# Chunk 14 of an MLP's second product as seven block products too, with two weight sums of chunks 13 and 14 made by accumulating transfers

## The chip, the core and the metric

The kernel runs on one NeuronCore of a Trainium2 chip. The metric is the device time of one execution in microseconds. TensorE (PE) multiplies 128x128 blocks into the banks of PSUM; VectorE (DVE) and ScalarE (ACT) do elementwise work; GpSimd (POOL) and SyncE (SP) issue transfers (DMA). Each engine takes its own instructions strictly in the order in which the program lists them, and waits at one whose inputs are not there.

## The reference

One layer of a decoder trunk over 256 rows of 1024: an input projection, a conformer convolution and a sparse attention, a cross attention, a squared-ReLU MLP and a last RMSNorm. What the change touches is the end:

```python
    hf = _rmsnorm(h, norm_ffn_g[l]) @ w_ff1[l]
    h = h + jnp.square(jax.nn.relu(hf)) @ w_ff2[l]
return _rmsnorm(h, norm_final_g)
```

`w_ff1` is 1024x4096, `w_ff2` 4096x1024, all float32.

## The kernel before

**Precision.** Every weight and activation is split into a high part (ACT copies it in a shorter float format, names `hi...`) and a low part (DVE subtracts the high one, names `lo...`). A product is three matmuls: high by high, high by low, low by high (`mm3`, line 382).

**The MLP.** It runs over 16 chunks of 256 hidden columns. For chunk c, the first product (`f1`, function `first`, line 1312) is made in two halves ("sides") of 128 columns into a bank `ps_f`; then ACT and DVE make the hidden part: relu, square, differences, high and low (`activation`, line 1225; tiles `ft` for the values, `fs` for high and low). The second product (`f2`) adds its share to the banks `ps_p`, named "1" to "7", which stay open over all chunks. The first product runs two chunks ahead of the second.

**Seven or eight block products.** The second product of a chunk is a 2x2 by 2x2 product of blocks (two groups of 128 rows, two of 128 hidden columns, two of 512 output columns), so eight block products of three 512-wide matmuls. For the chunks in `SEVEN` (1 to 13) it is done with seven, in Strassen's manner: the weights enter as four groups, "left" (two blocks as loaded), "last" (one block), "outer" and "inner" (two sums each), and the hidden part enters with three differences more. The weight sums (tiles `sums`) are made by DVE in `seven` (line 242): `outer()` adds one block to two others in one operation of 1024 elements, `inner(2)` and `inner(3)` add a block each, 512 elements, to what is there. `TERMS` (line 1304) says which weight block goes with which hidden part into which bank. At the end the banks are combined ("bank sums", tiles `comb`) and added to the rows `h_rm` ("residuals", `add_to` and `last_residual`).

**The end.** Chunks 14 and 15 (`JOINED` = 14) are done as eight plain products together, bank by bank, in `last_products` (line 1408), so that each bank is finished in turn: bank 2, 3, 4, then 5 and 1 with 256 columns each. Behind each bank DVE adds the residual, ACT squares and sums it (`last_squares`), and `last_norm` scales a block of 128 rows and issues its output.

**What sets the order.** The order is written by hand, as the program is recorded. Splits stand in a list of jobs (`last_jobs`, line 215): `split_high` records the next job's ACT part, `split_low` the next DVE part; `weights` calls both until the group that a product needs is there. Generators (`activation` among them) advance one step at each `tick()`; `done()` ticks until a hidden part is recorded. A job's high part may only be recorded while the pools `highs` and `lows` (6 tiles each) have room; some groups use tiles of the pool `t8` (12 tiles, taken in turn) in their place. Weights come in order on SP's queue (`load`, `fetch`): the next chunk's when a chunk's tile is released.

In names, the number in `hi80left` counts the stream's chunks: 78 is `f2` chunk 12, 80 chunk 13, 81 chunk 14 and 82 chunk 15.

## Time and profile before

| | |
|---|---|
| time, median of three runs (lowest to highest) | 501.92 us (501.77 to 502.3) |
| the profiled execution's own time, and its span | 501.92 us, 500.1 us |
| PE busy over the span | 490.9 us, 3120 matmuls |
| DVE busy | 465.4 us, 847 instructions |
| ACT busy | 349.1 us, 606 instructions |
| POOL busy | 30.7 us, 47 instructions |
| granted TensorE clock, mean | 0.997 |

The span goes from the first to the last instruction; the time of the run holds some work around it. Busy time of PE is modelled, since matmuls overlap, so stages are judged by what each engine waited for. In timelines a row gives the start, the busy time, the engine, the line, the operation with output and input, how many equal instructions it merges (x), and, in brackets, idle time of the engine before it with what ended it. Line 81 is the helper that records PE's and DVE's instructions (82 after the change), so tiles tell more than lines.

### The profile page before, as it was taken

To read this page: it belongs to the slowest core of one execution; us is meant where nothing else is said; L and a number is where in the kernel's file an instruction comes from. 1 tells how busy PE (TensorE), PEld (TensorE's weight loads), DVE (VectorE), ACT (ScalarE), POOL (GpSimd) and SP (SyncE) were. 2 spreads that over 40 slices of the span, in tenths; PEclk is the share of its full clock that TensorE was granted. 3 is DMA by queue.
4 is the path that set the end of the run, shared out by engine and by line. 5 is a ranking of instruction groups with operands and counts; after the bars stand their busy time and mean duration, and the time that the engine had idled before them with its cause. 6 is when DMAs were issued, how large, how long until landed. Compare 5 with 4: busy or idle time off the path is not lost.

```text
span 500.1 us, 8286 instructions
## 1 busy us (share of the span) xinstructions
PE 490.9 (98%) x3120; PEld 442.7 (89%) x3120; DVE 465.4 (93%) x847; ACT 349.1 (70%) x606; POOL 30.7 (6%) x47
## 2 busy tenths in 40 slices
PE   7999999999999999999999999999999999999995
PEld 5999998888888888888889999988999999999984
DVE  5999899999999789999988997799999999999996
ACT  7657777787856666767846567687777677777753
POOL 2002212221111100000000000000000000000000
PEclk9999999999999999999999999999999999999998
DMA  8959678899887653345655553766766456654412
GB/s 315 381 190 276 176 191 266 234 250 272 245 224 217 183 174 110 147 169 173 248 169 186 219 185 115 264 186 136 192 241 214 170 185 207 241 207 171 134 78 84
DMA packets 28376, 100.35 MB, mean 201 GB/s; under 512 B 10784, under 2 KB 11552, under 8 KB 19376
## 3 DMA queue, kind: packets, MB, share of 16 engines
q1 hardware_dynamic: 24416, 93.03, 54.7%
q0 software_dynamic: 3632, 6.59, 7.4%
q8 instruction: 24, 0.39, 0.3%
q10 hardware_dynamic: 288, 0.20, 0.1%
q14 instruction: 16, 0.13, 0.1%
HBM read 91.16 MB, written 1.05 MB: 184 GB/s over the span
## 4 chain that ended last, share of the span: by engine, by line
PE 85%; DVE 9%; ACT 3%; issue 1%; DMA 1%; POOL 0%; DVEq 0%; SPq 0%; ACTq 0%; POOLq 0%
PE ps_f L81 18%; PE ps_p L81 13%; PE ps_conv L81 10%; PE ps_ao L81 5%; PE ps_q L81 4%; PE ps_k L81 4%; PE ps_ga L81 4%; PE ps_gc L81 4%; PE ps_v L81 4%; PE ps_xo L81 3%; PE ps_qi L81 2%; PE ps_xk L81 2%; PE ps_xv L81 2%; DVE lo L81 2%; PE ps_xq L81 2%; DVE gc_t L81 1%
## 5 line engine op out<-in xcount | busy, mean ns | idle before, releaser
L81 DVE TENSOR_TENSOR lo<-raw,hi 128x1024 fp32r<-128x1024 f32 x133 | 161.2, 1215 | 3.4 <-ACT hi L295 3.0
L295 ACT ACTIVATE hi<-raw 128x1024 fp32r<-128x1024 f32 x133 | 138.5, 1047 | 2.4 <-DMA raw<-in_wst_dram 2.4
L81 PE MATMUL ps_f<-ff_p,hi 128*128 128x256 f32 (+1 forms) x464 | 92.5, 294 | 0.0
L81 PEld LDWEIGHTS ps_f<-ff_p,hi 128*128 128x128 f32 x464 | 75.3, 191 | 3.7
L81 DVE SCALAR_TENSOR_TENSOR acc<-u,cw,acc 128x234 f32<-128x234 f32 (+29 forms) x190 | 78.0, 461 | 0.3
L81 PE MATMUL ps_f<-ff_p,lo 128*128 128x256 f32 x256 | 71.3, 282 | 0.0
L81 PEld LDWEIGHTS ps_f<-ff_p,lo 128*128 128x128 f32 x256 | 48.9, 191 | 0.5
L81 PE MATMUL ps_conv<-n_p,hi 128*128 128x256 f32 x224 | 40.9, 285 | 0.0
L81 PEld LDWEIGHTS ps_conv<-n_p,hi 128*128 128x128 f32 x224 | 34.8, 192 | 0.9 <-issue 0.7
L81 PE MATMUL ps_conv<-n_p,lo 128*128 128x256 f32 x112 | 31.7, 283 | 0.0
L623 POOL DMA_DIRECT2D acc<-products x25 | 21.7, 867 | 125.6 <-ACT products L622 47.6
L273 ACT ACTIVATE inner<-sums 128x1024 fp32r<-128x1024 f32 x13 | 13.8, 1061 | 20.6 <-DVE sums L81 20.6
L81 PE MATMUL ps_q<-n_p,hi 128*128 128x512 f32 x64 | 23.6, 406 | 0.0
L81 PE MATMUL ps_k<-n_p,hi 128*128 128x512 f32 x64 | 23.5, 407 | 0.0
L81 PE MATMUL ps_ao<-o_p,hi 128*128 128x512 f32 x64 | 22.6, 401 | 0.0
L81 PE MATMUL ps_co<-u_p,hi 128*128 128x512 f32 (+1 forms) x80 | 22.2, 351 | 0.0
L81 PE MATMUL ps_mix<-mix_p,hi 128*128 128x512 f32 (+1 forms) x80 | 22.2, 351 | 0.0
L81 PE MATMUL ps_ga<-n_p,hi 128*128 128x512 f32 x64 | 22.0, 396 | 0.0
L81 PE MATMUL ps_gc<-n_p,hi 128*128 128x512 f32 x64 | 22.0, 396 | 0.0
L622 ACT ACTIVATE products<-u,cw 128x231 f32<-128x231 f32 (+24 forms) x50 | 21.9, 488 | 0.0
L81 PEld LDWEIGHTS ps_conv<-n_p,lo 128*128 128x128 f32 x112 | 21.5, 192 | 0.0
L81 PE MATMUL ps_p<-outer,fs 128*128 128x512 f32 x78 | 20.1, 393 | 0.0
(424 smaller groups left out, 1243.8 us busy)
## 6 DMA issues: line engine op xcount, KB each, us to landing
raw<-in_wst_dram SPq DMA_DIRECT2D x67, 1024.0 KB, 5.6
raw<-in_wst_dram SPq DMA_DIRECT2D x28, 512.0 KB, 4.4
acc<-products POOLq DMA_DIRECT2D x25, 256.0 KB, 6.8
x_rm<-in_x_dram SPq DMA_DIRECT2D x2, 512.0 KB, 4.1
mem_rm<-in_mem_dram SPq DMA_DIRECT2D x1, 1024.0 KB, 9.0
mem_t<-in_memt_dram SPq DMA_DIRECT2D x1, 1024.0 KB, 11.0
h_t<-in_xt_dram SPq DMA_DIRECT2D x1, 1024.0 KB, 7.1
raw_f<-in_wst_dram SPq DMA_DIRECT2D x1, 1024.0 KB, 9.5
```

The lines of the kernel that those rows point to most:

```text
L81: return fn(*args, **kwargs)
L273: act(hi, src, AF.Copy)
L295: act(hi, raw[:, ns], AF.Copy)
L622: act(prod[:, a, s:], u[:, t, : S - s], AF.Copy, scale=cw[:, t, TAPS - 1 - s : TAPS - s])
L623: nc.gpsimd.dma_start(acc[:, ts, :], prod, accum_op=ALU.add)
```

## The change

Chunk 14 joins `SEVEN`, and only chunk 15 is left for `last_products`. Chunk 13's and 14's products are interleaved: after chunk 15's first side come left, inner and outer of 13, then left, inner and outer of 14, then chunk 15's second side, then "last" of 13 and of 14. For both chunks the outer sums are no longer made by DVE: when the chunk's weights are fetched, POOL issues two transfers from DRAM, one that copies two blocks into `sums` and one that adds the third block to both (`accum_op`). The inner sums stay on DVE, in the order inner before outer. The high and low parts of the two chunks' sums go to the pools `highs` and `lows`. Chunk 15's raw weights get a `t8` tile of their own. The bank sums are spread: one ahead of "last" of 14, the others between the residuals of banks 2 and 3.

ACT's order ahead of the first products of chunk 14, before the change (`ft`, `fs` are hidden parts, `raw` weights as loaded, `both` chunk 15's weight parts; the rows go from the relu of chunk 14's second side on):

```order
L1203 ACTIVATE ft_5203<-ps_f_5255 128x256
L1232 ACTIVATE ft_5203<-ft_5203 128x512
L273 ACTIVATE outer_5288<-sums_5246 128x1024
L1210 ACTIVATE fs_5202<-ft_5203 128x512
L295 ACTIVATE hi_1_5301<-raw_3546 128x1024
L273 ACTIVATE inner_5318<-sums_5246 128x1024
L295 ACTIVATE hi_0_5327<-raw_5191 128x1024
L295 ACTIVATE hi_1_5335<-raw_5191 128x1024
L1203 ACTIVATE ft_5312<-ps_f_5333 128x256
L1217 ACTIVATE ft_5312<-ft_5312 128x256
L1391 ACTIVATE comb_5315<-ps_p_4008 128x512
```

and now, from chunk 13's inner high part on:

```order
L281 ACTIVATE hi80inner<-sums_5082 128x1024
L1212 ACTIVATE ft_5209<-ps_f_5260 128x256
L1241 ACTIVATE ft_5209<-ft_5209 128x512
L281 ACTIVATE hi80outer<-sums_5082 128x1024
L281 ACTIVATE hi81left<-raw_5194 128x1024
L281 ACTIVATE hi81inner<-sums_5196 128x1024
L1212 ACTIVATE ft_5319<-ps_f_5324 128x256
L1226 ACTIVATE ft_5319<-ft_5319 128x256
L281 ACTIVATE hi81outer<-sums_5196 128x1024
L1219 ACTIVATE fs_5208<-ft_5209 128x896
L1219 ACTIVATE fs_5318<-ft_5319 128x256
```

The inner high part of each chunk now stands ahead of the next relu and of the outer high part, and the hidden-14 part (`fs_5208`) is recorded behind chunk 14's outer high part.

DVE's order at the same place, before, from chunk 13's outer sum on:

```order
L81 TENSOR_TENSOR sums_5246<-raw_5080 128x1024
L81 TENSOR_TENSOR fs_5091<-ft_5092,fs_5091 128x896
L81 TENSOR_TENSOR lo80last<-raw_5080,hi80last 128x512
L81 TENSOR_TENSOR lo_0_5258<-raw_3546,hi_0_5257 128x1024
L81 TENSOR_TENSOR sums_5246<-sums_5246,raw_5080 128x512
L81 TENSOR_TENSOR outer_5288<-sums_5246,outer_5288 128x1024
L81 TENSOR_TENSOR sums_5246<-sums_5246,raw_5080 128x512
L81 TENSOR_TENSOR fs_5202<-ft_5203,fs_5202 128x512
L81 TENSOR_TENSOR lo_1_5302<-raw_3546,hi_1_5301 128x1024
L81 TENSOR_TENSOR inner_5318<-sums_5246,inner_5318 128x1024
L81 TENSOR_TENSOR lo_0_5328<-raw_5191,hi_0_5327 128x1024
L81 TENSOR_TENSOR lo_1_5336<-raw_5191,hi_1_5335 128x1024
```

and now, from the low part of chunk 15's first-side weights (`lo_0`) on:

```order
L82 TENSOR_TENSOR lo_0_5242<-raw_3546,hi_0_5241 128x1024
L82 TENSOR_TENSOR sums_5082<-sums_5082,raw_5080 128x512
L82 TENSOR_TENSOR fs_5094<-ft_5095,fs_5094 128x896
L82 TENSOR_TENSOR lo80left<-raw_5080,hi80left 128x1024
L82 TENSOR_TENSOR sums_5082<-sums_5082,raw_5080 128x512
L82 TENSOR_TENSOR lo80inner<-sums_5082,hi80inner 128x1024
L82 TENSOR_TENSOR ft_5209<-ft_5209 128x256
L82 TENSOR_TENSOR lo80outer<-sums_5082,hi80outer 128x1024
L82 TENSOR_TENSOR sums_5196<-sums_5196,raw_5194 128x512
L82 TENSOR_TENSOR ft_5209<-ft_5209 128x128
L82 TENSOR_SCALAR minus<-ms_ff 128x2
L82 TENSOR_TENSOR lo81left<-raw_5194,hi81left 128x1024
```

followed by:

```order
L82 TENSOR_TENSOR sums_5196<-sums_5196,raw_5194 128x512
L82 TENSOR_TENSOR ft_5209<-ft_5209 128x128
L82 TENSOR_TENSOR lo81inner<-sums_5196,hi81inner 128x1024
L82 TENSOR_TENSOR lo81outer<-sums_5196,hi81outer 128x1024
L82 TENSOR_TENSOR fs_5208<-ft_5209,fs_5208 128x896
L82 TENSOR_TENSOR fs_5318<-ft_5319,fs_5318 128x256
```

The sum of 1024 elements for chunk 13 is gone; two sums of 512 elements (`sums_5196`), three differences (`ft_5209`) and three lows of 1024 have come for chunk 14, and its hidden low (`fs_5208`, 896 in place of 512 elements) stands behind them.

DVE's order at the end, where banks are summed and added to the rows, before:

```order
L81 SCALAR_TENSOR_TENSOR h_rm<-comb_5315,ms_ff,h_rm 128x4x128
L81 TENSOR_TENSOR fs_5311<-ft_5312,fs_5311 128x256
L81 TENSOR_TENSOR comb_5315<-ps_p_4084,comb_5315 128x512
L81 TENSOR_TENSOR comb_5316<-ps_p_3912,comb_5315 128x512
L81 SCALAR_TENSOR_TENSOR h_rm<-comb_5316,ms_ff,h_rm 128x4x128
L81 TENSOR_TENSOR comb_5315<-ps_p_4070,comb_5315 128x512
L81 TENSOR_TENSOR comb_5316<-ps_p_4070,comb_5316 128x512
L81 SCALAR_TENSOR_TENSOR h_rm<-comb_5315,minus,h_rm 128x4x128
L81 SCALAR_TENSOR_TENSOR h_rm<-comb_5316,ms_ff,h_rm 128x4x128
L81 SCALAR_TENSOR_TENSOR h_rm<-ps_p_3898,ms_ff,h_rm 128x4x128
L81 SCALAR_TENSOR_TENSOR h_rm<-ps_p_3908,ms_ff,h_rm 128x4x128
L81 SCALAR_TENSOR_TENSOR ss_o<-ss_o,table 128x1
```

and now:

```order
L82 SCALAR_TENSOR_TENSOR h_rm<-comb_5322,ms_ff,h_rm 128x4x128
L82 TENSOR_TENSOR comb_5322<-ps_p_4084,comb_5322 128x512
L82 TENSOR_TENSOR fs_5318<-ft_5319,fs_5318 128x256
L82 TENSOR_TENSOR comb_5323<-ps_p_3912,comb_5322 128x512
L82 SCALAR_TENSOR_TENSOR h_rm<-comb_5323,ms_ff,h_rm 128x4x128
L82 SCALAR_TENSOR_TENSOR h_rm<-ps_p_3898,ms_ff,h_rm 128x4x128
L82 TENSOR_TENSOR comb_5322<-ps_p_4070,comb_5322 128x512
L82 TENSOR_TENSOR comb_5323<-ps_p_4070,comb_5323 128x512
L82 SCALAR_TENSOR_TENSOR h_rm<-comb_5322,minus,h_rm 128x4x128
L82 SCALAR_TENSOR_TENSOR h_rm<-ps_p_3908,ms_ff,h_rm 128x4x128
L82 SCALAR_TENSOR_TENSOR ss_o<-ss_o,table 128x1
L82 SCALAR_TENSOR_TENSOR h_rm<-comb_5323,ms_ff,h_rm 128x4x128
```

Ahead of the second hidden-15 low now stand one residual and one bank sum; the other three sums and two residuals stand between the residuals of bank 2 (`ps_p_3898`) and bank 3 (`ps_p_3908`).

The diff:

```diff
--- before.py
+++ after.py
@@ -57,8 +57,9 @@
 HALVES = 6
 EARLY = (3,)
 WHOLE = (("conv", 0),)
-SEVEN = tuple(range(1, 14))
-JOINED = 14
+SEVEN = tuple(range(1, 15))
+JOINED = 15
+ADDED = (13, 14)
 FIRST = STREAM.index(("f1", 2))
 BY_HALVES = ()
 
@@ -163,8 +164,8 @@
 
     prepared, whole, elsewhere = {}, {}, set()
     order = [c for c, key in enumerate(STREAM) if key[0] != "f1" or key[1] < 3]
-    early = set(EARLY)
-    raw_of, landed = {}, set()
+    early = {*EARLY, STREAM.index(("f2", 15))}
+    raw_of, landed, sums_of = {}, set(), {}
     high_jobs, low_jobs = [], []
 
     def fetch(c, raw, parts=1, only=None):
@@ -186,6 +187,11 @@
         key = STREAM[c]
         fetch(c, t8(f"raw{c}", F32, (P, N_CHUNK)) if c in early else raws.tile([P, N_CHUNK], F32, tag="raw", name=f"raw{c}"),
               2 if key in BY_HALVES else parts)
+        if key[0] == "f2" and key[1] in ADDED:
+            sums = sums_of[c] = t8(f"sums{c}", F32, (P, 4, 512))
+            nc.gpsimd.dma_start(sums[:, 0:2, :], wst[INDEX[key]].rearrange("p (j n) -> p j n", j=4)[:, 0:4:3, :])
+            nc.gpsimd.dma_start(sums[:, 0:2, :], wst[INDEX[key]].rearrange("p (j n) -> p j n", j=4)[:, 1:2, :].to_broadcast([P, 2, 512]),
+                                accum_op=ALU.add)
         if key in WHOLE:
             whole[key] = raw_of[c].rearrange("p (k n) -> p k n", k=2 * KT)
         elif c < FIRST:
@@ -218,13 +224,12 @@
             return jobs_of(STREAM.index((kind, i)))
 
         jobs = []
-        for i in range(JOINED):
+        for i in range(JOINED - 2):
             one, two = of("f1", i + 2), of("f2", i)
             half = len(two) // 2
-            jobs += [one[0], *two[:half], one[1], *two[half:]] if i < JOINED - 1 else [*two[:2], one[0], two[2], one[1], two[3]]
-        for i in range(JOINED, 16):
-            jobs += of("f2", i)
-        return jobs
+            jobs += [one[0], *two[:half], one[1], *two[half:]]
+        one, (l13, z13, o13, i13), (l14, z14, o14, i14) = of("f1", 15), of("f2", 13), of("f2", 14)
+        return jobs + [one[0], l13, i13, o13, l14, i14, o14, one[1], z13, z14, *of("f2", 15)]
 
     class Stage:
 
@@ -247,9 +252,12 @@
         def flat():
             return raw_of[c].rearrange("p (j n) -> p j n", j=4)
 
-        sums = []
+        sums, added = [], key[1] in ADDED
 
         def outer():
+            if added:
+                sums.append(sums_of[c])
+                return
             sums.append(t8(f"sums{c}", F32, (P, 4, 512)))
             dve.tensor_tensor(out=sums[0][:, 0:2, :], in0=flat()[:, 0:4:3, :],
                               in1=flat()[:, 1:2, :].to_broadcast([P, 2, 512]), op=ALU.add)
@@ -263,7 +271,7 @@
         def stage(name, src_of, n, steps=()):
             def high():
                 src = src_of()
-                if steps:
+                if steps and not added:
                     both = t8(f"{name}{c}", F32R, (P, 2, 2, 512))
                     hi, lo = both[:, 0], both[:, 1]
                 else:
@@ -278,11 +286,12 @@
 
                 low_jobs.append(low)
 
-            return Stage((*key, name), high, steps, not steps, (key, 0))
+            return Stage((*key, name), high, steps, added or not steps, (key, 0))
 
         return [stage("left", lambda: b()[:, :, 0, :], 2), stage("last", lambda: flat()[:, 3:4, :], 1),
-                stage("outer", lambda: sums[0][:, 0:2, :], 2, (outer,)),
-                stage("inner", lambda: sums[0][:, 2:4, :], 2, (lambda: inner(2), lambda: inner(3)))]
+                stage("outer", lambda: sums[0][:, 0:2, :], 2, () if added else (outer,)),
+                stage("inner", lambda: sums[0][:, 2:4, :], 2,
+                      (outer, lambda: inner(2), lambda: inner(3)) if added else (lambda: inner(2), lambda: inner(3)))]
 
     def high(key, c, ns, q, last):
         raw, n = raw_of[c], ns.stop - ns.start
@@ -1368,12 +1377,10 @@
         h = h_rm[:, lo // P : hi // P, 1 - rb, :]
         dve.scalar_tensor_tensor(out=h, in0=by_tiles(ps), scalar=scales[:, 1 - rb : 2 - rb], in1=h, op0=ALU.mult, op1=ALU.add)
 
-    for c in range(JOINED):
+    for c in range(JOINED - 2):
         hidden.append(Hidden(c + 2))
         x, later = hidden[c], hidden[c + 2]
         wide = c not in SEVEN and c != 5
-        if c == JOINED - 1:
-            break
         first(later, 0, wide)
         x.done()
         if c in (0, 1):
@@ -1382,21 +1389,26 @@
         first(later, 1, wide)
         half_of(x, 1)
     hg = t8("hg", F32, (P, 2, D))
+    hidden.append(Hidden(15))
+    x, y, later = hidden[13:]
     r, b = r2[0], banks
     minus = small.tile([P, 2], F32, tag="minus", name="minus")
+    dve.tensor_scalar(minus, r, -1.0, None, ALU.mult)
     v, e = (w2(f"comb{j}") for j in range(2))
+    first(later, 0, False)
     x.done()
-    half_of(x, 0)
-    first(later, 0, False)
-    act(v, b["1"], AF.Copy)
-    seventh(x, "outer")
-    split_ahead()
+    for z, name in ((x, "left"), (x, "inner"), (x, "outer"), (y, "left"), (y, "inner"), (y, "outer")):
+        z.done()
+        if name == "outer" and z is y:
+            act(v, b["1"], AF.Copy)
+        seventh(z, name)
+        tick()
+    first(later, 1, False)
+    add_to(0, 0, 512, v, r)
+    seventh(x, "last")
     tick()
-    first(later, 1, False)
-    dve.tensor_scalar(minus, r, -1.0, None, ALU.mult)
-    seventh(x, "inner")
-    add_to(0, 0, 512, v, r)
-    split_ahead()
+    dve.tensor_tensor(out=v, in0=b["6"], in1=v, op=ALU.subtract)
+    seventh(y, "last")
     tick()
     ws = {}
     for c in range(JOINED, 16):
@@ -1411,20 +1423,20 @@
             mm3(ps, *hidden[c].row(k, rb), w[0][:, 0, cols], w[1][:, 0, cols], fresh and c == JOINED and k == 0,
                 c == 15 and k == 1)
 
-    dve.tensor_tensor(out=v, in0=b["6"], in1=v, op=ALU.subtract)
     dve.tensor_tensor(out=e, in0=b["5"], in1=v, op=ALU.add)
     add_to(0, 512, D, e, r)
+    zero_c = table
+    nc.gpsimd.memset(zero_c, 0.0)
+    last_products(0, 0, b["2"])
+    last_residual(0, b["2"], 0, 512)
+    last_squares(0, 0, 0, 512)
     dve.tensor_tensor(out=v, in0=b["7"], in1=v, op=ALU.add)
     dve.tensor_tensor(out=e, in0=b["7"], in1=e, op=ALU.add)
     add_to(1, 0, 512, v, minus)
+    last_products(0, 1, b["3"])
+    last_residual(0, b["3"], 512, D)
+    last_squares(0, 1, 512, D)
     add_to(1, 512, D, e, r)
-    zero_c = table
-    nc.gpsimd.memset(zero_c, 0.0)
-    for hf in range(2):
-        ps = b["23"[hf]]
-        last_products(0, hf, ps)
-        last_residual(0, ps, 512 * hf, 512 * hf + 512)
-        last_squares(0, hf, 512 * hf, 512 * hf + 512)
     last_norm(0, 1)
     last_products(1, 0, b["4"])
     last_residual(1, b["4"], 0, 512)
```

## The prediction

> **What bounds the kernel now.** I read the page first, then busy time by stage for the end of the span, then the timeline of each engine there.
>
> ```profile
> span 500.1 us, 8286 instructions
> ...
> PE 85%; DVE 9%; ACT 3%; issue 1%; DMA 1%; POOL 0%; DVEq 0%; SPq 0%; ACTq 0%; POOLq 0%
> ```
>
> Over the whole span the chain that ended last is TensorE (PE). The change touches the last 35 us alone, so it is the stage that counts. Busy time by stage (columns: stretch, its length, busy us of PE, PEld, DVE, ACT, POOL with their instructions, granted clock, DMA share, GB/s):
>
> ```profile
> 466.00:484.00 18.00, 18.00 (x115) 16.33 (x114) 16.94 (x21) 13.71 (x21) 0.00 (x0) 1.00 0.34 122
> ...
> 494.20:497.40 3.20, 0.01 (x1) 0.00 (x0) 2.07 (x7) 1.87 (x6) 0.00 (x0) 1.00 0.03 9
> 497.40:500.10 2.70, 0.00 (x0) 0.00 (x0) 0.00 (x0) 0.00 (x0) 0.00 (x0) 0.50 0.49 183
> ```
>
> From 466 to 484 PE never stops, but VectorE (DVE) is busy 16.94 of 18.00 us: it has 1.06 us to give. So PE bounds the stage with DVE right behind it. The timeline of PE gives its pieces (start, busy time, operation):
>
> ```profile
> 472.45 0.39 PE L81 MATMUL ps_p<-hi80left,fs 128*128 128x512 f32 x1
> ...
> 474.49 0.40 PE L81 MATMUL ps_f<-ff_p,hi 128*128 128x256 f32 x2
> ...
> 477.37 1.55 PE L81 MATMUL ps_p<-outer,fs 128*128 128x512 f32 x6
> ...
> 488.45 0.39 PE L81 MATMUL ps_p<-hi,fs 128*128 128x512 f32 x1
> ...
> 491.17 0.28 PE L81 MATMUL ps_p<-hi,fs 128*128 128x256 f32 x1
> ...
> 492.61 0.28 PE L81 MATMUL ps_p<-hi,fs 128*128 128x256 f32 x1
> ```
>
> A half of chunk 15's first product takes 2.88 us (474.49 to 477.37). Twelve 512-wide matmuls take 2.72 (488.45 to 491.17), 0.227 each, so a group of six is 1.36; twelve 256-wide ones take 1.44, 0.12 each. PE ends at 492.61 + 1.44 = 494.05. DVE's timeline gives the time from one start to the next for each size:
>
> ```profile
> 463.46 0.29 DVE L81 TENSOR_TENSOR ft<-ft 128x128 f32<-128x128 f32 x1
> 463.67 1.22 DVE L81 TENSOR_TENSOR outer<-sums,outer 128x1024 fp32r<-128x1024 f32 x1
> ...
> 466.33 1.23 DVE L81 TENSOR_TENSOR lo80left<-raw,hi80left 128x1024 fp32r<-128x1024 f32 x1
> 467.47 1.22 DVE L81 TENSOR_TENSOR sums<-raw 128x1024 f32<-128x1024 f32 x1
> 468.61 1.08 DVE L81 TENSOR_TENSOR fs<-ft,fs 128x896 fp32r<-128x896 f32 x1
> 469.61 0.68 DVE L81 TENSOR_TENSOR lo80last<-raw,hi80last 128x512 fp32r<-128x512 f32 x1
> ...
> 479.87 2.36 DVE L81 TENSOR_TENSOR both<-raw,both 128x1024 fp32r<-128x1024 f32 x2 [0.95 <-ACT both L295]
> ...
> 482.48 0.16 DVE L81 TENSOR_SCALAR minus<-ms_ff 128x2 f32<-128x2 f32 x1
> 482.55 0.75 DVE L81 SCALAR_TENSOR_TENSOR h_rm<-comb,ms_ff,h_rm 128x512 f32<-128x512 f32 x1
> 483.21 0.42 DVE L81 TENSOR_TENSOR fs<-ft,fs 128x256 fp32r<-128x256 f32 x1
> 483.55 1.41 DVE L81 TENSOR_TENSOR comb<-ps_p,comb 128x512 f32<-128x512 f32 x2
> 484.99 0.75 DVE L81 SCALAR_TENSOR_TENSOR h_rm<-comb,ms_ff,h_rm 128x512 f32<-128x512 f32 x1
> 485.66 1.28 DVE L81 TENSOR_TENSOR comb<-ps_p,comb 128x512 f32<-128x512 f32 x2
> 486.86 0.74 DVE L81 SCALAR_TENSOR_TENSOR h_rm<-comb,minus,h_rm 128x512 f32<-128x512 f32 x1
> ...
> 488.18 1.41 DVE L81 SCALAR_TENSOR_TENSOR h_rm<-ps_p,ms_ff,h_rm 128x512 f32<-128x512 f32 x2
> ...
> 490.91 1.42 DVE L81 SCALAR_TENSOR_TENSOR hg<-h_rm,rs_o,g_out 128x512 f32<-128x512 f32 x2
> ```
>
> Steps: 1.14 for 1024 elements, 1.00 for 896, 0.60 for 512 (0.72 where the next one reads the result), 0.34 for 256, 0.21 for 128, 0.66 for a residual, 0.07 for minus. From ACT's timeline:
>
> ```profile
> 470.32 0.63 ACT L1232 ACTIVATE ft<-ft 128x512 f32<-128x512 f32 x1
> 470.86 1.05 ACT L273 ACTIVATE outer<-sums 128x1024 fp32r<-128x1024 f32 x1
> ...
> 477.98 0.42 ACT L1217 ACTIVATE ft<-ft 128x256 f32<-128x256 f32 x1
> 478.31 0.58 ACT L1391 ACTIVATE comb<-ps_p 128x512 f32<-128x512 f32 x1
> 478.79 2.00 ACT L295 ACTIVATE both<-raw 128x1024 fp32r<-128x1024 f32 x2
> ...
> 481.83 0.38 ACT L1203 ACTIVATE ft<-ps_f 128x256 f32<-128x256 f32 x1 [0.74 <-PE ps_f L81]
> 482.24 0.42 ACT L1217 ACTIVATE ft<-ft 128x256 f32<-128x256 f32 x1
> 482.69 0.42 ACT L1210 ACTIVATE fs<-ft 128x256 fp32r<-128x256 f32 x1
> ```
>
> A high part is 1.05 (0.95 to the next start), relu 0.41 to its square, the square 0.54 (512) or 0.33 (256) to the next, 0.45 to what reads it. DVE starts 0.03 after the ACT result that it waits for (478.79 + 1.05, then 479.87).
>
> **The change part by part.** *PE.* Chunk 14 had eight products, 18 matmuls of 512 and 12 of 256: 4.09 + 1.44 = 5.53 us. Seven products are 21 of 512: 4.77. Gain **0.76 us**, if PE is never kept waiting.
>
> *DVE and ACT.* Two transfers replace chunk 13's outer sum (one step of 1.14). Chunk 14 adds two inner sums (1.20), three differences of its hidden part (0.76), a hidden low of 896 for one of 512 (0.40), and weight lows of three times 1024 and one 512 for two of 1024 (1.74). Net **+2.96 us** of DVE, where 1.06 is free. And PE now runs six product groups back to back (8.2 us) where it had a half of chunk 15's first product between 13's groups; all their inputs must be ready earlier.
>
> *The queue up to chunk 14's first product.* The orders are those shown in the section on the change. Unchanged up to the DVE start at 466.33, DVE then holds: f1 low 466.33, sum for 13 467.47, hidden-13 low 468.07, left low 469.07, second sum 470.21, which ends at 470.89. ACT has stood at 13's inner high, which reads that sum: 470.92 to 471.97. DVE: inner low 472.00, difference 473.14, idle from 473.48. ACT: relu 471.87, square 472.28, outer high 472.82 to 473.87. DVE: outer low 473.90, sum for 14 475.04, difference 475.64, minus 475.85, left low 475.92, second sum 477.06 to 477.74. ACT has again stood: 14's inner high 477.77 to 478.82, relu and square of hidden 15 from 478.72, outer high 479.46 to 480.51. DVE: inner low 478.85, outer low 480.54, hidden-14 low 481.68, which ends 1.09 later, at 482.77. Behind each of the two ACT waits stand the relu, the square and the hidden-14 high, though their own inputs were ready.
>
> PE: half of chunk 15 from 472.45 to 475.33, three groups of 13 to 479.41, whose lows (470.2, 473.1, 475.0) are there when PE comes to them. Then 14's left product needs the hidden-14 parts. The high (behind the outer high, from 480.41, at most 1.05) lets two matmuls go at about 481.4, the third needs the low: 482.80 in place of 479.41 + 0.45 = 479.86. **PE waits 2.94 us.** Then four matmuls (0.91), two groups (2.72), the second half of chunk 15 (2.88): 489.31. Both "last" products (1.36): 490.67. Chunk 15's own 18 and 12 matmuls (5.52): PE ends at 496.19, 2.14 later than now.
>
> *The tail.* Today DVE makes the four bank sums and the residuals from 483.21 on, beside 11 us of PE's last products; its last steps need nothing that PE is late with. Afterwards the same work begins when hidden 15 is done, with half those products left. In the rows PE leaves its half at 481.63 (0.20 ahead of the relu at 481.83); now 489.31. Relu 489.51, square 489.92, high 490.37, low 490.81 (high 0.41, and 0.03). Queued on DVE: low 0.34, sum 0.72, residual 0.66, bank 2's 0.66 (at 492.53; the bank is there at about 492.2), two sums 1.20, residual 0.66: bank 3's residual starts at 495.05. Today it starts at 488.18 + 0.66 = 488.84, and the scaled row block at 490.91, 2.07 later; the moved residual (0.66) fits into that wait. So the scaling starts at 497.12, **6.21 later than now**. From there on the rows are the same, DVE is behind PE throughout (the last residual now at 494.48, then about 500.7, against a PE done at 496.2), so the end moves by 6.21.
>
> *The transfers.* The four are issued by POOL, which has nothing else by then. No row shows an accumulating load of 512 KB. Nearest rows (issue by issue: size, us to landing):
>
> ```profile
> raw<-in_wst_dram SPq DMA_DIRECT2D x67, 1024.0 KB, 5.6
> raw<-in_wst_dram SPq DMA_DIRECT2D x28, 512.0 KB, 4.4
> acc<-products POOLq DMA_DIRECT2D x25, 256.0 KB, 6.8
> ```
>
> Bounds for one: 4.4 (a plain load of this size) and 13.6 (twice 6.8); a doubled load adds 1.2 us, so I take 6.8 + 1.2 = 8.0. Their tiles come free when PE has finished chunk 9's outer and chunk 10's inner products:
>
> ```profile
> 438.03 1.55 PE L81 MATMUL ps_p<-outer,fs 128*128 128x512 f32 x6
> ...
> 449.97 1.52 PE L81 MATMUL ps_p<-inner,fs 128*128 128x512 f32 x6
> ```
>
> So 13's pair starts at 439.6 and lands at 455.6, wanted at 467.47; 14's starts at 451.5 and lands at 467.5, wanted at 475.04. At 8.0 and below they cost nothing; at 13.6, 14's pair (behind 13's second issue) lands at 481.3, 6.3 late. The added traffic beside the weight loads I put at nothing, since DMA is 0.34 busy; its other end is 1 us.
>
> Sum: 500.1 + 6.2 = 506.3 us of span. The profiled run took 501.92, 1.8 us around its span, and is the median of the runs; 501.92 + 6.2 = **508.1 us**.
>
> **The rivals.** *DVE keeps up, not slower* (chance 0.06): if hidden 14's low were ready by 479.86 and the bank sums hid beside PE, the end would follow PE: 0.76 off, and at most the 0.27 by which DVE's last residual (494.48) trails PE's end, 500.9 to 501.2. It decides at 2.94 us of DVE and ACT time; the order gives no sign of it, and 2.96 us more work in a stage with 1.06 free speaks against it. *Tail alone* (0.06): PE is not held, through an ACT queue that flows, but the sums still come after hidden 15: 508.1 - 2.9 = 505.2. *Late transfers* (0.05): above 11 us each, 14's pair passes 475.04; at 13.6 the end is 514.4. *The clock drops* (0.05): PE stops at 494.05 and the granted clock is 0.50 only from 497.40, so 3.3 us of idle are needed; my gap is 2.0, two matmuls, then 1.0. A wait grown by over 1.3 us would halve the speed for about as long, 1.7 us: 509.8. [...] That the change leaves something undone I rule out: the order shows 21 matmuls for chunk 14 and one outer sum fewer.
>
> **How the numbers follow.** Forecast 0.78, with 507.4 to 508.9 as its own range (rounding of some 25 steps, and 1 us for slower loads). To hold 8 in 10 and the nearer rivals the range reaches from 505.1 (tail alone) to 509.9 (clock); late transfers and "not slower" stay out. 0.2% is 1.0 us, about what a measurement tells from no change: faster 0.02 and same 0.04 share the first rival, with 500.9 and 501.2 on the two sides of that line; slower 0.94.
>
> **What would show it.** PE idle about 2 us and then 1 us ahead of chunk 14's left product, released by ACT and then DVE (hidden 14); ACT idle about 3 us twice ahead of the two inner highs, released by DVE's sums; no DVE wait on a DMA; PE ending near 496, and DVE's residual of bank 3 near 495 with the output after 502. I am wrong if PE runs through from 472 to 493, if DVE waits for the transfers, or if the last output still follows PE's end by under 3 us.

## The result, and the profile after

| | before | changed |
|---|---|---|
| time, median (lowest to highest) | 501.93 us (501.77 to 502.3), 4 runs | 510.05 us (508.51 to 510.13), 4 runs |
| ratio of the times, 95% interval | | 1.0144 [1.0112, 1.0176] |
| the profiled execution's own time, and its span | 501.92 us, 500.1 us | 508.51 us, 506.7 us |
| matmuls; DVE instructions | 3120; 847 | 3111; 853 |

The changed kernel is slower by 8.1 us. Its four times are 508.51, 509.99, 510.10 and 510.13, and the profiled execution is the first: what stands in its trace explains 6.6 us, and the other 1.5 us is something that this execution did not have. From the page of the changed kernel, its span and the row of the granted clock in 40 slices:

```profile
span 506.7 us, 8286 instructions
...
PEclk9999999999999999999999999999999999999997
```

Busy time by stage of the changed kernel (columns as in the prediction's first such view):

```profile
466.00:484.00 18.00, 15.51 (x90) 13.13 (x89) 15.07 (x20) 12.13 (x18) 0.00 (x0) 1.00 0.32 127
484.00:496.40 12.40, 12.40 (x73) 10.95 (x71) 10.46 (x17) 4.38 (x9) 0.00 (x0) 1.00 0.00 0
496.40:501.25 4.85, 0.19 (x2) 0.00 (x0) 4.35 (x9) 1.93 (x7) 0.00 (x0) 1.00 0.30 108
```

From 466 to 484 PE was busy all 18.00 us before and now 15.51. DVE, which now has more to do, is also *less* busy there than before (15.07 against 16.94), and so is ACT (12.13 against 13.71). All three lose busy time in this stage, because they wait for each other, as the waits in their rows show. PE's timeline shows where:

```profile
479.29 0.39 PE L82 MATMUL ps_p<-hi80outer,fs 128*128 128x512 f32 x1
481.48 0.50 PE L82 MATMUL ps_p<-hi81left,fs 128*128 128x512 f32 x1 [1.80 <-ACT fs L1219]
481.82 0.40 PE L82 MATMUL ps_p<-lo81left,fs 128*128 128x512 f32 x1
482.90 0.73 PE L82 MATMUL ps_p<-hi81left,fs 128*128 128x512 f32 x2 [0.69 <-DVE fs L82]
...
490.92 5.67 PE L82 MATMUL ps_p<-both,fs 128*128 128x512 f32 x30
```

Ahead of chunk 14's left product PE waits for the hidden-14 high part (ACT), does two matmuls, and waits for its low part (DVE). ACT's timeline:

```profile
471.01 1.06 ACT L281 ACTIVATE hi80inner<-sums 128x1024 fp32r<-128x1024 f32 x1 [2.85 <-DVE sums L82]
...
477.86 1.06 ACT L281 ACTIVATE hi81inner<-sums 128x1024 fp32r<-128x1024 f32 x1 [2.96 <-DVE sums L82]
...
489.74 0.38 ACT L1212 ACTIVATE ft<-ps_f 128x256 f32<-128x256 f32 x1 [3.63 <-PE ps_f L82]
```

And DVE's:

```profile
472.10 1.23 DVE L82 TENSOR_TENSOR lo80inner<-sums,hi80inner 128x1024 fp32r<-128x1024 f32 x1 [1.13 <-ACT hi80inner L281]
...
478.95 1.23 DVE L82 TENSOR_TENSOR lo81inner<-sums,hi81inner 128x1024 fp32r<-128x1024 f32 x1 [0.93 <-ACT hi81inner L281]
480.62 1.23 DVE L82 TENSOR_TENSOR lo81outer<-sums,hi81outer 128x1024 fp32r<-128x1024 f32 x1 [0.44 <-ACT hi81outer L281]
481.76 1.42 DVE L82 TENSOR_TENSOR fs<-ft,fs 128x896 fp32r<-128x896 f32 x2
...
491.05 0.43 DVE L82 TENSOR_TENSOR fs<-ft,fs 128x256 fp32r<-128x256 f32 x1 [1.80 <-ACT fs L1219]
...
492.78 0.75 DVE L82 SCALAR_TENSOR_TENSOR h_rm<-ps_p,ms_ff,h_rm 128x512 f32<-128x512 f32 x1
...
495.30 0.75 DVE L82 SCALAR_TENSOR_TENSOR h_rm<-ps_p,ms_ff,h_rm 128x512 f32<-128x512 f32 x1
...
497.36 1.41 DVE L82 SCALAR_TENSOR_TENSOR hg<-h_rm,rs_o,g_out 128x512 f32<-128x512 f32 x2
```

Twice ACT stands for nearly 3 us (2.85 and 2.96) at an inner high part, because DVE's second sum stands behind DVE's own queue; then DVE stands for about 1 us (1.13 and 0.93), because the inner low part needs that high part. The hidden-14 parts, which PE needs first, are recorded behind all of this on both engines. At the end, PE starts its last product at 490.92 and finishes it, by the forecast's time per matmul, 5.52 later (the row with its modelled last end has 5.67), near 496.4, 2.4 later than before. But the scaling of the first row block starts at 497.36, 6.45 later than the 490.91 of before: DVE's work behind hidden 15 comes late by more than PE does. (The section on the change has the order of that work wrong in one point, which its listing has right: only two sums and one residual stand between the residuals of banks 2 and 3; one sum and one residual stand ahead of bank 2's, and one residual behind bank 3's.)

The two pairs of transfers on POOL (first the copy, then the adding one; below them the transfers' rows for each in the same order, with size and time from issue to landing):

```profile
439.96 0.79 POOL L192 DMA_DIRECT2D sums<-in_wst_dram  x1 [142.38 <-PE ps_p L82]
444.58 1.22 POOL L193 DMA_DIRECT2D sums<-in_wst_dram  x1 [3.84 <-DMA sums<-in_wst_dram]
451.88 0.76 POOL L192 DMA_DIRECT2D sums<-in_wst_dram  x1 [6.09 <-PE ps_p L82]
458.03 1.20 POOL L193 DMA_DIRECT2D sums<-in_wst_dram  x1 [5.39 <-DMA sums<-in_wst_dram]
```

```profile
sums<-in_wst_dram POOLq DMA_DIRECT2D x1, 512.0 KB, 4.3
sums<-in_wst_dram POOLq DMA_DIRECT2D x1, 512.0 KB, 9.5
sums<-in_wst_dram POOLq DMA_DIRECT2D x1, 512.0 KB, 5.9
sums<-in_wst_dram POOLq DMA_DIRECT2D x1, 512.0 KB, 8.1
```

They start within 0.4 us of the forecast 439.6 and 451.5. A copy takes 4.3 and 5.9 us, an adding transfer 9.5 and 8.1. The second pair has landed at 458.03 + 8.1 = 466.1, 9 us ahead of the 475.13 at which DVE adds to it, and no instruction of DVE or ACT waits for a transfer.

### The profile page after: what moved, and what is told of

It is laid out like the page before. It is cut to its first block, busy times and chain, and to the rows that moved or that the text cites. A ratio compares the mean times of both kernels' runs of the same rounds, so it can differ in the third digit from the quotient of the medians.

```text
span 506.7 us, 8286 instructions
## 1 busy us (share of the span) xinstructions
PE 491.0 (97%) x3111; PEld 442.1 (87%) x3111; DVE 468.6 (92%) x853; ACT 351.1 (69%) x608; POOL 34.6 (7%) x51
## 4 chain that ended last, share of the span: by engine, by line
PE 83%; DVE 9%; ACT 5%; issue 2%; DVEq 0%; ACTq 0%
PE ps_f L82 17%; PE ps_p L82 12%; PE ps_conv L82 9%; PE ps_ao L82 4%; PE ps_q L82 4%; PE ps_k L82 4%; PE ps_ga L82 4%; PE ps_gc L82 4%; PE ps_v L82 4%; PE ps_xo L82 3%; PE ps_qi L82 2%; PE ps_xk L82 2%; PE ps_xv L82 2%; DVE lo L82 2%; PE ps_xq L82 2%
## 5 line engine op out<-in xcount | busy, mean ns | idle before, releaser
L82 DVE TENSOR_TENSOR lo<-raw,hi 128x1024 fp32r<-128x1024 f32 x131 | 159.4, 1219 | 3.5 <-ACT hi L304 3.0
L304 ACT ACTIVATE hi<-raw 128x1024 fp32r<-128x1024 f32 x131 | 136.7, 1048 | 2.3 <-PE ps_v L82 1.6
L281 ACT ACTIVATE inner<-sums 128x1024 fp32r<-128x1024 f32 x12 | 12.7, 1062 | 20.2 <-DVE sums L82 20.2
L1212 ACT ACTIVATE ft<-ps_f 128x256 f32<-128x256 f32 x26 | 9.8, 378 | 15.5 <-PE ps_f L82 15.5
```

The costliest lines, as they stand in the source:

```text
L82: return fn(*args, **kwargs)
L281: act(hi, src, AF.Copy)
L304: act(hi, raw[:, ns], AF.Copy)
L1212: act(t, ps, AF.Relu)
```

## The experiments

Nine runs were made, each beside the kernel before. All times are medians of device microseconds.

| run | what it is | time (lowest to highest) | ratio to before, 95% |
|---|---|---|---|
| e1_after_again | the changed kernel, unchanged | 509.98 (508.48 to 511.17) | 1.0156 [1.0135, 1.0176] |
| e2_gap_filled | changed, with matmuls in the gap | 508.48 (508.47 to 508.64) | 1.0128 [1.0113, 1.0143] |
| e3_hidden_earlier | changed, hidden 14 ahead of 13's products | 507.59 (507.44 to 507.88) | 1.0109 [1.0092, 1.0126] |
| e4_side_between | changed, second side between 13 and 14 | 506.58 (506.4 to 506.73) | 1.009 [1.0075, 1.0105] |
| e5_side_between_no_sums | e4 without the bank sums | 503.76 (503.7 to 504.16) | 1.0036 [1.0024, 1.0049] |
| e6_before_no_sums | before without the bank sums | 501.72 (501.56 to 501.89) | 0.9993 [0.9984, 1.0002] |
| e7_sums_on_dve | changed, outer sums on DVE | 511.6 (511.16 to 511.96) | 1.019 [1.0176, 1.0204] |
| e8_spread_alone | before, bank sums spread | 501.79 (501.63 to 505.83) | 1.0003 [0.9988, 1.0018] |
| e9_transfers_alone | before, transfers for chunk 13 | 502.02 (501.85 to 502.37) | 1.0002 [0.9993, 1.0011] |

### The changed kernel again

The edit: none. The question is what makes 510.0 of the 508.5 that its profile explains.

> The changed kernel once more, unchanged. Three of its four runs took about 510.1 us at a mean granted clock of 0.989 to 0.992, the profiled one 508.51 at 0.995. Theory (clock): the idle of PE ahead of chunk 14's left product (1.8 and 0.7 us in the profile, with two matmuls between) halves the granted clock for a stretch in most executions. Then the times fall in two groups, near 508.5 and near 510.1, and a profile of the second group shows a stretch at 0.50 behind that idle, with the matmuls there at about twice their time. Rival (no clock): the 1.5 us lie elsewhere (slower loads, a DVE wait on a transfer), and the clock stays at 1.00 until PE has ended.

The times were 511.17, 509.97, 508.48 and 509.99, and the profiled execution was the slowest, so this trace shows what the first one did not have. PE's timeline of this run:

```profile
481.44 0.50 PE L82 MATMUL ps_p<-hi81left,fs 128*128 128x512 f32 x1 [1.80 <-ACT fs L1219]
481.79 0.58 PE L82 MATMUL ps_p<-lo81left,fs 128*128 128x512 f32 x1
482.87 1.22 PE L82 MATMUL ps_p<-hi81left,fs 128*128 128x512 f32 x2 [0.50 <-DVE fs L82]
...
493.57 5.67 PE L82 MATMUL ps_p<-both,fs 128*128 128x512 f32 x30
```

The same matmuls, released at the same times and by the same engines as in the first trace (481.48 and 482.90 there), but two of them are listed with 1.22 us in place of 0.73, and the last product starts at 493.57, 2.65 later. Busy time and granted clock (the column behind POOL's) of this run, cut where the clock changes:

```profile
478.42:481.83 3.41, 1.60 (x8) 0.98 (x6) 2.47 (x3) 3.38 (x7) 0.00 (x0) 1.00 0.01 2
481.83:488.66 6.83, 6.33 (x16) 4.59 (x15) 6.73 (x9) 4.23 (x6) 0.00 (x0) 0.50 0.00 0
488.66:502.31 13.65, 10.58 (x64) 9.29 (x62) 8.67 (x16) 3.15 (x9) 0.00 (x0) 1.00 0.05 18
```

From 481.83 on, between PE's two waits, the clock is halved (0.50) for 6.83 us, then it is full (1.00) for 13.65 us, and it is halved again from 502.31 on, after the end of PE's work. 6.83 is 2 and 13.65 is 4 times 3.413 us: the three changes of this trace lie whole multiples of 3.41 us apart. Places at this distance from a change are called marks below. In the stretch between the last two marks ahead of the drop PE was busy for 1.60 of 3.41 us. Here is the changed kernel's first trace, which kept its clock, cut at the marks that follow from the one place where its clock falls, at the end (501.25), if the distance of e1 holds in it too:

```profile
477.36:480.77 3.41, 2.32 (x11) 1.58 (x9) 2.04 (x4) 2.88 (x5) 0.00 (x0) 1.00 0.01 2
480.77:484.18 3.41, 2.01 (x8) 1.36 (x9) 3.41 (x4) 3.41 (x6) 0.00 (x0) 1.00 0.00 0
```

There the same idle time falls on both sides of such a mark, so that neither stretch had less than 2.01 us of busy time. The author's reading is that the same kernel gives times 2.7 us apart (508.48 and 511.17) in this way: the work is the same, the place of the marks is not. It rests on these two traces. Whether it is PE's busy time between two marks that decides, or the longest idle piece between them, these traces do not tell apart: the piece of 1.80 us lies whole between two marks in e1 and is cut by a mark in the first trace.

### Matmuls in the gap

Twelve matmuls of operands that have long been there, into a bank that nobody reads, ahead of chunk 14's left product:

```diff
+        if name == "left" and z is y:
+            spare = ps_mm("ps_spare")
+            for n in range(12):
+                pe.matmul(spare, f2.high(0)[:, 0:P], f2.both(0), start=True, stop=True)
```

> The changed kernel, with 12 matmuls of 512 columns (2.7 us) into a free bank, never read, put on PE ahead of chunk 14's left product, where it is idle. By my theory they take the place of the wait alone and move nothing else, and PE is never idle for long: the clock holds, all runs within 0.3 us of 508.5, none near 510.1. Rival (no clock): most runs stay near 510.1. If the wait of PE were not set by hidden 14, the end would be up to 2.7 us later than 508.5.

PE's timeline of this run:

```profile
479.47 2.88 PE L82 MATMUL ps_spare<-ff_p 128*128 128x512 f32 x12
...
482.85 0.74 PE L82 MATMUL ps_p<-hi81left,fs 128*128 128x512 f32 x2
...
490.91 5.67 PE L82 MATMUL ps_p<-both,fs 128*128 128x512 f32 x30
```

The added work took no time: the left product's third matmul starts at 482.85 and the last product at 490.91, as in the first trace, and the granted clock is 1.00 in every stretch from 466 to 500. All four times (508.47 to 508.64) are now within 0.2 us of 508.5, where the changed kernel gave 508.5 in one execution of four. So the idle time itself, by way of the clock, costs **1.5 us** of the median (509.98 - 508.48), and the rest of the loss is untouched by it.

### Hidden 14 recorded earlier

```diff
     x.done()
+    y.done()
```

> The changed kernel, with the hidden part of chunk 14 finished ahead of chunk 13's products in the program, so that its high and low stand ahead of chunk 14's inner high on ACT and DVE. Theory: PE's wait falls from 2.5 to under 2 us in three smaller pieces (hidden 14, then the weights of inner and outer), the second low of hidden 15 starts 0.8 us earlier, the end too: 507.7 us at full clock. With idle in smaller pieces the clock may hold more often. Rival (the order of hidden 14 doesn't matter, DVE's total work does): no earlier than 508.5.

Waits between 466 and 507 in this run (who waits, for whom, us in total, times, longest):

```profile
PE ps_p L82 <- ACT fs L1219: 0.9, 1, 0.9
...
PE ps_p L82 <- DVE fs L82: 0.4, 1, 0.4
```

In the changed kernel these two waits were 1.80 and 0.69. Recording hidden 14 ahead of chunk 13's products takes about half of PE's wait away, leaves no clock drop in the trace (1.00 in every stretch from 466 to 497) and four times within 0.44 us of each other, and gives 507.59. Against e2, which differs from it in the place of the wait but not in the clock, it is 0.9 us. The queue ahead of the left product is therefore really what holds PE, but most of the loss stays.

### The second side between 13 and 14

Chunk 15's second half of the first product, 2.9 us of PE work, goes back between chunk 13's products and chunk 14's, where the kernel before has such a piece:

```diff
-        return jobs + [one[0], l13, i13, o13, l14, i14, o14, one[1], z13, z14, *of("f2", 15)]
+        return jobs + [one[0], l13, i13, o13, one[1], l14, i14, o14, z13, z14, *of("f2", 15)]
...
+        if name == "left" and z is y:
+            first(later, 1, False)
...
-    first(later, 1, False)
```

> The changed kernel, with the second side of chunk 15's first product put between chunk 13's and chunk 14's products. Theory (tail): PE no longer waits and ends at 493.4, 0.7 us before the kernel before, and yet the end stays late, since DVE's bank sums and residuals can start only when chunk 14's products are done: 506.4 us, 4.2 to 4.7 over before. Rival (the PE wait is the whole loss): with the wait gone the end follows PE, 501.2 us.

PE's timeline of this run, and DVE's:

```profile
488.13 5.67 PE L82 MATMUL ps_p<-both,fs 128*128 128x512 f32 x30
```

```profile
480.57 1.23 DVE L82 TENSOR_TENSOR lo81inner<-sums,hi81inner 128x1024 fp32r<-128x1024 f32 x1 [1.13 <-ACT hi81inner L281]
...
491.04 0.74 DVE L82 SCALAR_TENSOR_TENSOR h_rm<-ps_p,ms_ff,h_rm 128x512 f32<-128x512 f32 x1
...
493.56 0.75 DVE L82 SCALAR_TENSOR_TENSOR h_rm<-ps_p,ms_ff,h_rm 128x512 f32<-128x512 f32 x1
...
495.62 1.41 DVE L82 SCALAR_TENSOR_TENSOR hg<-h_rm,rs_o,g_out 128x512 f32<-128x512 f32 x2
```

PE waits for nothing any more; its last product starts at 488.13 and ends, with the same time per matmul, 5.52 later, at 493.65, which is 0.4 *earlier* than in the kernel before (494.05). All of this trace's PE rows are later by some 0.35 from the start of the kernel on (the first long run of matmuls starts at 9.09, before at 8.73), so PE has gained the whole 0.76 us of matmuls that the change was to save. And yet the kernel is 4.5 us slower than before, because from 480.57 to 495 no idle time is listed ahead of any DVE row: bank 2's residual comes at 491.04 where it came at 488.18, and the scaling 4.71 later than before. A faster PE and a slower end: here the end belongs to DVE.

### Without the bank sums

The bank sums, their copy on ACT and their residuals are left out (their shares are missing from the output), once from e4 and once from the kernel before. The core of both edits:

```diff
-    add_to(0, 0, 512, v, r)
...
-    dve.tensor_tensor(out=v, in0=b["6"], in1=v, op=ALU.subtract)
...
-    dve.tensor_tensor(out=e, in0=b["5"], in1=v, op=ALU.add)
-    add_to(0, 512, D, e, r)
...
-    dve.tensor_tensor(out=v, in0=b["7"], in1=v, op=ALU.add)
-    dve.tensor_tensor(out=e, in0=b["7"], in1=e, op=ALU.add)
-    add_to(1, 0, 512, v, minus)
...
-    add_to(1, 512, D, e, r)
```

> The kernel with the second side put between (506.58 us), without the bank sums and their residuals: ACT's copy of bank 1, four sums and four residuals on DVE, 5.04 us there, are left out, so the output lacks these shares. It splits the late tail. Theory (sums): DVE's sums behind chunk 14's products are the whole of it, then the end follows PE (which ends at 493.4) and falls to about 501.2 us. Rival (bank order): part of it is that bank 3 is finished 2.4 us later than before (about 490.9, before 488.5), since chunk 14's products are no longer done bank by bank with chunk 15's, and everything from the scaling of the first row block on hangs on bank 3: then 503.8 us, so 2.8 of sums and 1.9 of bank order.

> The kernel before, without the same bank sums and residuals (the output lacks these shares). Theory: there the sums lie beside PE's last products, so leaving them out gives next to nothing, 0.2 us: 501.8. Rival (the sums cost their DVE time wherever they stand): up to 5 us less, near 497.

In the kernel before the sums cost nothing that can be measured (501.72, ratio 0.9993 with 1 inside the interval): all of them lie beside PE. In e4 they cost 506.58 - 503.76 = **2.8 us**. But 1.7 us more than before stay without them, which is what the expectation's rival (bank order) said, not its theory. DVE's timeline of e5, and that of e6 behind it:

```profile
489.26 0.75 DVE L82 SCALAR_TENSOR_TENSOR h_rm<-ps_p,ms_ff,h_rm 128x512 f32<-128x512 f32 x1 [1.61 <-PE ps_p L82]
490.62 0.75 DVE L82 SCALAR_TENSOR_TENSOR h_rm<-ps_p,ms_ff,h_rm 128x512 f32<-128x512 f32 x1 [0.61 <-PE ps_p L82]
...
492.69 1.42 DVE L82 SCALAR_TENSOR_TENSOR hg<-h_rm,rs_o,g_out 128x512 f32<-128x512 f32 x2
```

```profile
488.64 0.75 DVE L81 SCALAR_TENSOR_TENSOR h_rm<-ps_p,ms_ff,h_rm 128x512 f32<-128x512 f32 x1 [1.97 <-PE ps_p L81]
...
490.71 1.42 DVE L81 SCALAR_TENSOR_TENSOR hg<-h_rm,rs_o,g_out 128x512 f32<-128x512 f32 x2
```

Now DVE waits for PE at banks 2 and 3, and the scaling still comes 1.78 later than the 490.91 of before. In the kernel before, chunks 14 and 15 end bank by bank, with twelve matmuls for each of banks 2, 3 and 4, and bank 4 begins at 488.45, 5.6 us ahead of PE's end. With chunk 14 as seven products, all of its groups are done ahead of chunk 15's products, and only chunk 15's six matmuls for each bank are left to do bank by bank: bank 2 and bank 3 are ready at most 4.2 and 2.8 us ahead of PE's end (24 and 18 matmuls' worth: 5.52 - 1.36, and 5.52 - 2.72). The first row block's residual, square and scaling then find less of PE's work to lie beside. e5 and e6 beside each other show it: in both the sums are gone and DVE waits for PE at bank 3, its residual starts at 490.62 and at 488.64, the scaling follows 2.07 later in both, and the times are 2.04 us apart. So that price lies in the order in which PE closes the banks and not in the order of DVE's work. Whether another order of chunk 15's products could lower it was not tried.

### The sums back on DVE

```diff
-            nc.gpsimd.dma_start(sums[:, 0:2, :], wst[INDEX[key]].rearrange("p (j n) -> p j n", j=4)[:, 0:4:3, :])
-            nc.gpsimd.dma_start(sums[:, 0:2, :], wst[INDEX[key]].rearrange("p (j n) -> p j n", j=4)[:, 1:2, :].to_broadcast([P, 2, 512]),
-                                accum_op=ALU.add)
...
+                dve.tensor_tensor(out=sums[0][:, 0:2, :], in0=flat()[:, 0:4:3, :],
+                                  in1=flat()[:, 1:2, :].to_broadcast([P, 2, 512]), op=ALU.add)
```

> The changed kernel without the four transfers: the outer sums of chunks 13 and 14 are made by DVE (two more operations of 1024 elements, 2.3 us), ahead of the inner ones. Theory: DVE sets when chunk 14's first product can start, so most of it lands on the end: PE idle 3.0 and 1.2 us, the end 1.65 us later at full clock, 510.2, and with the longer idle the clock drops in all runs: 511.5 to 513. Rival (the transfers disturb more than they save): no later than the changed kernel's 510.0.

It is slower still, by 1.6 us against the changed kernel's 510.0. Its trace shows a longer wait of PE ahead of the left product (and one of 0.6 for ACT ahead of chunk 15's second side, which the changed kernel does not have), and a clock drop too (0.50 for 3.41 us). Waits, and busy time cut at the clock's changes:

```profile
PE ps_p L82 <- ACT fs L1218: 2.6, 1, 2.6
```

```profile
480.51:483.92 3.41, 0.73 (x2) 0.30 (x2) 2.97 (x3) 3.38 (x6) 0.00 (x0) 1.00 0.01 2
483.92:487.33 3.41, 2.90 (x7) 2.32 (x8) 3.41 (x6) 3.41 (x6) 0.00 (x0) 0.50 0.00 0
487.33:504.40 17.07, 12.12 (x71) 10.57 (x69) 13.30 (x24) 4.59 (x14) 0.00 (x0) 1.00 0.09 31
...
497.59:501.01 3.42, 1.86 (x14) 1.58 (x13) 2.99 (x7) 1.02 (x3) 0.00 (x0) 1.00 0.00 0
```

So the transfers do what they are for: they take work from DVE where DVE is late, and are worth 1.6 us *inside this change*, counted with the clock's part in both kernels. The clock is seen here with a single halved stretch of 3.41 us, behind one in which PE was busy for 0.73 of 3.41 us, and followed by 17.07 us at 1.00, five times that. The last row is the stretch between two marks in which PE ends: behind its 1.86 us of busy time the clock was still at 1.00, up to 504.40.

### One part alone, in the kernel before

Bank sums spread as in the change (the residuals and squares of banks 2 and 3 moved between the sums):

```diff
+    last_products(0, 0, b["2"])
+    last_residual(0, b["2"], 0, 512)
+    last_squares(0, 0, 0, 512)
     dve.tensor_tensor(out=v, in0=b["7"], in1=v, op=ALU.add)
...
+    last_products(0, 1, b["3"])
+    last_residual(0, b["3"], 512, D)
+    last_squares(0, 1, 512, D)
     add_to(1, 512, D, e, r)
```

> The kernel before with one part of the change alone: the bank sums spread around the first residuals. Theory: 0.2 us earlier at most (bank 2's and bank 3's residuals stand ahead of some sums), 501.8, not to be told from no change. Rival (the spreading is what makes the tail late): over 503.

And chunk 13's outer sums by adding transfers:

```diff
+        if key == ("f2", 13):
+            sums = sums_of[c] = t8(f"sums{c}", F32, (P, 4, 512))
+            nc.gpsimd.dma_start(sums[:, 0:2, :], wst[INDEX[key]].rearrange("p (j n) -> p j n", j=4)[:, 0:4:3, :])
+            nc.gpsimd.dma_start(sums[:, 0:2, :], wst[INDEX[key]].rearrange("p (j n) -> p j n", j=4)[:, 1:2, :].to_broadcast([P, 2, 512]),
+                                accum_op=ALU.add)
...
+            if c in sums_of:
+                sums.append(sums_of[c])
+                return
```

> The kernel before, with one thing of the change alone: the two outer sums of chunk 13 are made by adding transfers instead of two operations of DVE. Theory: in the kernel before PE never waits for DVE ahead of chunk 13's products, so the two operations taken from DVE there (1.14 us) bring nothing: 502.0 us, between 501.6 and 502.4, and PE ends at 494.05 as before. Rival, that the transfers' 2 MB beside the weights' loads delay a block of weights: PE has a wait on DMA of some tenths to 1 us, and the time is 502.4 to 503.0. Rival, that DVE's time at this place does reach the end: 500.9 us.

(The change's outer sum is one operation of 1024 elements; the expectation counts it as two. Its "2 MB" of transfers are two of 512 KB, as the rows give them.) Neither changes the time by an amount that can be measured: 1.0003 [0.9988, 1.0018] and 1.0002 [0.9993, 1.0011]. (Ten of e8's eleven executions took at most 502.03; one took 505.83, and its reason is not known.) 1.14 us taken from DVE bring nothing where PE never waits for DVE, and the transfers' traffic costs nothing there (502.02 against 501.93 beside it). Both parts that work against DVE's load are harmless and useless alone; the loss comes with the rest of the change, chunk 14's seven products and their place among chunk 13's, which no run separates.

## Why the prediction was right, and where it was not

**Direction and mechanism: right, shown for executions that keep their clock.** The 508.1 us forecast holds for a full clock. The profiled execution, which kept it, took 508.51; only two of eight did, so it was luck that the trace could be laid beside the forecast row by row. The median lies 1.95 above the forecast; 1.5 of it is the clock's part, below. Step by step, forecast and then measured in the first trace: the second sums let ACT begin at 470.92 and 477.77 (471.01 and 477.86), the inner lows at 472.00 and 478.85 (472.10 and 478.95), the outer low of 14 at 480.54 (480.62), the left product's third matmul at 482.80 (482.90), "last" done at 490.67 (490.92), the second hidden-15 low at 490.81 (491.05), bank 2's residual at 492.53 (492.78), bank 3's at 495.05 (495.30), the scaling at 497.12 (497.36). The queue order and a row's own duration were enough for that. Of the 0.25 us that were missed by "last", 0.10 were there at the left product's third matmul, and most of the rest arose in the four matmuls behind it, which took 1.03 (482.90 to 483.93) and not 0.91. e3 shows that this queue holds PE: with hidden 14 recorded earlier the waits halve.

**PE's gain of 0.76 us: right.** In e4, without waits, PE ends 0.4 earlier than before in a trace that runs 0.35 late from its start. The gain never reaches the end of the kernel.

**DVE's net 2.96 us with 1.06 free: right in kind.** It is DVE's queue, and not PE's end, that the kernel's end follows: in e4 PE is earlier, DVE has no listed wait from 480.57 to 495, and the kernel is 4.5 us slower. How much of this the 2.96 us alone are worth no run measures. The rival "tail alone" priced a kernel whose PE never waits at 505.2, as the forecast less PE's wait of 2.9. e4, which is such a kernel (with the second side at another place), took 506.58. The wait of PE and the lateness of DVE overlap, so that subtracting the one does not leave the other: DVE's own queue is late even when PE is not.

**The tail, 6.21 us: right in size (6.45), incomplete in reason.** The prediction gave it to the bank sums that begin when hidden 15 is done. The runs split the tail of e4, 4.5 us, in two: 2.8 for the sums and their residuals, and 1.7 that stay without them. That banks 2 and 3 close later, nearer to PE's end (2.0 us between e5 and e6), stood in the sum only as a time at which a bank "is there", not as a cost of its own.

**The transfers: right in what counts.** 8.0 us were taken for each; the pairs took 4.3 + 9.5 and 5.9 + 8.1, 14 us a pair in place of 16. No instruction of DVE or ACT waits for them, and the traffic of one pair costs nothing that e9 can tell (1.0002).

**The clock: wrong in its condition, near in its price.** This is the step that failed. The prediction's rival had it that "3.3 us of idle are needed", from the time between PE's end and the fall of the clock in the kernel before, that the gap of 2.0 us, two matmuls and 1.0 us was therefore safe, and gave the drop a chance of 0.05. In fact the forecast gap itself, not a longer one, halved the clock: the drop is seen in e1's trace behind just this gap (1.80 us idle, then 0.50 of full clock from 481.83 on, for 6.83 us), and filling the gap (e2) takes the times to 508.5 in all four executions, against one in four without. Of the eight executions of the changed kernel two stood at 508.5, five at 510.0 to 510.1 and one at 511.17; only the first kind and the last were traced, and that the group at 510.0 had one halved stretch of 3.41 us is inferred from e7's trace and from the distance of 1.5 us. The median of 510.05 lies 0.15 above the range, at the time that this rival was priced (509.8). That the price came near is in part luck: it was worked out for a longer wait, which did not come. The reading of the row was at fault: the 3.35 us from PE's end at 494.05 to the fall at 497.40 are not a length of idle time that has to pass, since in e1 the clock fell at 481.83 behind an idle piece of 1.80 us. They fit a stop and the *next mark* behind it (from 493.99 to 497.40, 3.41 us, PE was busy for 0.21 us), but the trace of the kernel before has one change of the clock only and does not show marks.

Nor did a stretch between two marks have to be empty: behind 1.60 us of busy time in 3.41 the clock was halved in e1, and behind 0.73 in e7, while behind 1.86 in e7 and 2.01 in the first trace it stayed at 1.00.

**Left open.** Why the halved stretch lasts once 3.41 us (e7) and once 6.83 us (e1) the runs do not tell: PE was busy for 2.90 us in the first 3.41 of it in e7, and for 2.91 in e1. Chunk 14 as seven products without any interleaving with chunk 13 was not tried. And no version was found that beats the kernel before: the nearest, with all products in the changed form and PE free of waits (e4), is 4.5 us slower, 1.7 of which would stay even if the sums were free.

## What to carry to other kernels

Before saving matmuls, add up what the saving costs the elementwise engines *in that stage* and at the end of the kernel: 0.76 us of PE were bought with 2.96 us of DVE, where 1.06 were free, and with a last row block that had less of PE's work to lie beside. Where two engines feed each other (a high part on one, a low part on the other), look at what stands *behind* the instruction that waits: the operation that PE needed first had its own inputs and stood behind two such waits (2.85 and 2.96 us on ACT), and recorded earlier it cut PE's waits of 1.80 and 0.69 us to 0.9 and 0.4. And do not take a short PE gap for safe by its length alone: with the same wait of 1.80 us the granted clock stayed at 1.00 in one trace of the changed kernel and fell to 0.50 for 6.83 us in the other. Matmuls whose result nobody reads, put into the gap, cost nothing (the last product at 490.91 against 490.92) and gave 1.5 us back.

## What the runs showed of the hardware that was not expected

- The granted clock changed at distances of 6.83 and 13.65 us (e1) and of 3.41 and 17.07 us (e7), all whole multiples of 3.41. Behind 3.41 us in which PE was busy for 1.60 us it was at 0.50 for 6.83 us (e1), and behind 0.73 us for 3.41 us (e7). Behind stretches with 1.86 (e7), 2.01 and 2.32 us of busy time (the first trace) it was at 1.00.
- With a gap of some 2 us ahead of chunk 14's left product the same kernel took 508.48 to 511.17 us, in groups 1.5 us apart (508.5 and 510.0) and one time above them, where the kernel before (501.8 to 502.24 beside e1 and e2) and the filled kernel (508.47 to 508.64) stay within 0.5 us. That it depends on where the gap falls between the marks is the author's reading of two traces, and no run moved the gap against them.
- An adding transfer of 512 KB into on-chip memory took 9.5 and 8.1 us beside the weights' loads (9.4 in e9), where the plain copy of the same size just ahead of it took 4.3 and 5.9.
